# A decoder block on one core: second score passes over 128 partitions, three vectors loaded as rows, modulation sums kept in another order

## The chip, the core and the metric

The kernel runs on one core of one Trainium2 chip. The core has TensorE (PE: matmuls, with the weight loads, PEld, listed apart), VectorE (DVE), ScalarE (ACT), GpSimd (POOL) and SyncE (SP, which here only issues transfers). Each engine works through its own instructions in order; semaphores hold an instruction until what it needs is there. The metric is the time of one execution on the device in microseconds (us), from the first to the last instruction and what the launch adds.

## The reference

One layer on x of 512 tokens and width 2048, all in float32:

```
mod = silu(c) @ W_ada + b_ada              # six vectors of 2048: shift, scale, gate for mixer and MoE
h   = RMSNorm(x) * (1 + scale_mix) + shift_mix
q_a k_a v_a | q_b k_b v_b f_b = h @ W_in
o_a = sliding-window attention (128), 16 query heads on 4 key heads, ALiBi, sinks
o_b = forgetting attention, 16 heads: logits + cum[q] - cum[k], cum = cumsum(log sigmoid(f_b))
x   = x + gate_mix * ([RMSNorm(o_a) | RMSNorm(o_b)] @ W_out)
h2  = RMSNorm(x) * (1 + scale_moe) + shift_moe
x   = x + gate_moe * MoE(h2)               # top 1 of 4 groups, then top 2 of 8 experts
y   = RMSNorm_final(x)
```

Heads are 64 wide. The scores have to be as exact as float32 makes them, so the kernel cuts operands into a high part (the type fp32r, which PE takes in one pass) and a low part (what is left).

## The kernel before

**Start (0 to 155 us).** `load_x` brings x in four transfers of 1 MB on SP's queue; `rms_x` makes the row sums of squares on ACT and DVE. ACT's queue brings c, two parts of b_ada and norm_mix_g (lines 97 to 102), the latter three with `cols8`, that is, as runs of two numbers for each partition. Eight units of `gemv` then multiply pieces of W_ada (tiles `raws`, six buffers) with silu(c) on DVE, POOL and PE, and give the shift and scale of the mixer (`shA`, `scA`), 256 columns at a time; the queries and keys of the first heads are accumulated behind them.

**The turn (145 to 186 us).** `evac_k` takes each bank of keys out of PSUM. The high part goes to both halves of the partitions (`dst`, four ACT copies of 64 partitions), the low part to one half alone (`low`, two DVE subtractions): head e of a pair has its low part on partitions 64e to 64e+63. `evac_q` puts the high part of q on the same half and its low part on the other. Then the values of the sliding-window heads are projected (tiles `va`), and the logarithms of the forget gates are taken and summed (`log_forget`, `cumulate`, `cumulated`).

**Attention (186 to 750 us).** `attend` goes through units. A unit of the sliding-window heads (`swa_units`, 32 units) is one head and half of the tokens: two blocks of queries; a unit of the forgetting heads (`fox_units`, 64) is one head and one block of queries. `a1` makes the scores: a first matmul of q (128 partitions: high and low part) with the high part of k, and a second of q with the low part of k, over the 64 partitions `rows`. In a fox unit a third matmul in bf16 adds the causal mask. `a2` scales the probabilities of the unit before, `b` transposes those of two units before, `c` multiplies with the values. For each fox head `pre` spreads the cumulated logarithms over the partitions with a matmul (tile `bp`) over 48 partitions. Between these steps, `fill.take(step)` writes matmuls of the remaining projections (`transposed`, `natural`) into PE's order, and with them, at a fixed rate, the steps of a side work, `ada_side`: for the sections 3 and 4 of W_ada (shift and scale of the MoE, eight sums) and 2 (gate) it multiplies pieces of W_ada (tiles `raw`, five buffers, shared with the weights of the projections) with silu(c): row j=0 of a piece on DVE (`ga`, line 608), row j=1 on ACT and POOL (`gb`, lines 610 and 611). `finish` sums over the partitions by matmuls with `ones` (tile `cm`): for sections 3 and 4 four matmuls whose stationary operand is every fourth column of the sum, since the result is wanted with column p*4+j at partition p.

**Output and MoE (750 to 1950 us).** W_out, the gates of section 5, routing, then 16 pairs of experts. Nothing in it is changed but the place of one small transpose and of its two loads: `norm_a` put `grow` (the gains of the output norms) through PE into `gout`; `small_loads` loads it on SP's queue.

The order is written out by hand throughout (a manual schedule). Each transfer signals one of eight semaphores (DMAHW0 to DMAHW7) in turn, and a later transfer on the same one waits until the earlier has landed.

## Time and profile before

| | |
|---|---|
| median of 3 runs | 1953.34 us (1949.9 to 1963.09) |
| the profiled execution | 1952.11 us, of which the span 1950.4 us |
| PE busy | 1853.0 us (95%) |
| DVE busy | 1085.3 us (56%) |
| ACT busy | 824.5 us (42%) |
| POOL busy | 347.7 us (18%) |
| HBM read | 566.78 MB |

The span runs from the first to the last instruction. "Busy" of PE counts from a matmul's start to its modelled end, and matmuls overlap, so a PE that is 100% busy may still run at half of its pace: the distance from one start to the next is what a matmul costs in a chain of them. Rows of the timeline give start and duration in us; an "x8" is eight instructions merged into one row, from the first start to the last end.

### The profile page before, as it was taken

The numbers are of one execution on the slowest core, as the hardware profiler recorded it, in microseconds if no ns is written. First come the engines' busy times: TensorE is split into PE (matmuls) and PEld (weight loads), VectorE is DVE, ScalarE is ACT, GpSimd is POOL, SyncE is SP. The second block draws the span as 40 slices with busy tenths as digits, with TensorE's granted clock in tenths as the row PEclk, the third lists the DMA queues.
The fourth block names the chain that finished last, engine by engine and source line by source line (L and its number), as shares of the span: only waits on it lengthen the run. The fifth ranks groups of instructions, "written<-read, shape, count | busy, mean of one in ns | idle before, by whom it ended". The sixth has DMA issues, their size and how long they took to land.

```text
span 1950.4 us, 25464 instructions
## 1 busy us (share of the span) xinstructions
PE 1853.0 (95%) x9287; PEld 1122.2 (58%) x9287; DVE 1085.3 (56%) x2046; ACT 824.5 (42%) x1710; POOL 347.7 (18%) x281
## 2 busy tenths in 40 slices
PE   4999999999999999997999999999999999999994
PEld 2668777787777777875344444444444444444442
DVE  5775777767777555656344445444544445444435
ACT  4445655555555433444433334333333333333313
POOL 2440433443344321453000000000000000000000
PEclk9999999999999999998999999999999999999998
DMA  9994454565566332767799998999999999999994
GB/s 313 327 290 106 147 159 139 173 205 159 170 198 191 105 119 79 237 219 308 287 421 379 383 380 353 385 411 406 422 416 412 412 410 421 406 415 414 410 410 151
DMA packets 211749, 572.73 MB, mean 294 GB/s; under 512 B 25721, under 2 KB 113817, under 8 KB 162977
## 3 DMA queue, kind: packets, MB, share of 16 engines
q1 hardware_dynamic: 207632, 570.96, 78.4%
q8 instruction: 75, 1.23, 0.3%
q10 hardware_dynamic: 3984, 0.07, 0.1%
q14 instruction: 58, 0.47, 0.1%
HBM read 566.78 MB, written 4.19 MB: 293 GB/s over the span
## 4 chain that ended last, share of the span: by engine, by line
PE 84%; DVE 7%; ACT 3%; DMA 2%; issue 2%; POOL 1%; ACTq 1%; SPq 0%; DVEq 0%; POOLq 0%
PE pg L1371 12%; PE pu L1371 11%; PE y L1394 11%; PE xg L1351 7%; PE o L1416 5%; PE qp L216 3%; PE qp L217 3%; PE qp L218 3%; PE xe L1359 2%; DMA raw<-in_w_ada_dram 2%; PE vb L216 2%; PE vb L217 2%; PE vb L218 2%; PE sb L776 1%; DVE sum L291 1%
## 5 line engine op out<-in xcount | busy, mean ns | idle before, releaser
L1419 DVE SCALAR_TENSOR_TENSOR x<-o,wpair,x 128x512 f32<-128x512 f32 x240 | 163.5, 744 | 239.2 <-PE o L1416 239.2
L1371 PE MATMUL pg<-w,cw 128*64 128x512 f32 x1008 | 231.6, 602 | 1.2 <-ACT cw L1361 1.2
L1371 PE MATMUL pu<-w,cw 128*64 128x512 f32 x1008 | 227.3, 592 | 0.0
L611 POOL TENSOR_TENSOR gb<-gb,raw 128x512 f32<-128x512 f32 x112 | 163.1, 1456 | 288.8 <-ACT raw L610 237.3
L1394 PE MATMUL y<-w,cw 128*64 128x512 f32 x960 | 210.0, 594 | 0.1
L1361 ACT ACTIVATE cw<-xe,shM,scM 128x128 f32<-128x128 f32 x256 | 96.2, 456 | 248.0 <-PE xe L1359 247.8
L1340 DVE SCALAR_TENSOR_TENSOR wlo<-x,rs,whi 128x512 fp32r<-128x512 f32 x252 | 172.3, 746 | 43.3 <-ACT whi L1334 43.3
L1334 ACT ACTIVATE whi<-x,rs 128x512 fp32r<-128x512 f32 x256 | 163.4, 711 | 1.1 <-DVE rs L136 1.1
L1371 PEld LDWEIGHTS pu<-w,cw 128*64 128x64 f32 x1008 | 73.4, 137 | 142.9 <-issue 141.9
L1371 PEld LDWEIGHTS pg<-w,cw 128*64 128x64 f32 x1008 | 67.1, 137 | 130.3 <-issue 123.5
L1394 PEld LDWEIGHTS y<-w,cw 128*64 128x64 f32 x960 | 67.4, 137 | 129.3 <-issue 123.6
L1400 DVE TENSOR_TENSOR cw<-y,gm 128x512 f32<-128x512 f32 x60 | 41.5, 692 | 152.9 <-PE y L1394 150.8
L178 DVE TENSOR_TENSOR wlo_s<-raw,whi_s 128x512 fp32r<-128x512 f32 x96 | 85.6, 892 | 73.3 <-ACT whi_s L177 73.2
L608 DVE SCALAR_TENSOR_TENSOR ga<-raw,csil,ga 128x512 f32<-128x512 f32 x112 | 108.8, 972 | 24.8 <-DMA raw<-in_w_ada_dram 24.4
L1351 PE MATMUL xg<-wlo,cr 128*128 128x512 f32 x256 | 104.7, 409 | 7.5 <-DVE wlo L1340 7.5
L1351 PE MATMUL xg<-whi,cr 128*128 128x512 f32 x256 | 107.3, 419 | 1.4 <-DVE cr L1314 1.4
L216 PE MATMUL qp<-hT_hi,whi_s 128*128 128x512 f32 x256 | 108.5, 424 | 0.0
L1352 ACT ACTIVATE cw<-xg 128x512 f32<-128x512 f32 x64 | 38.2, 598 | 165.9 <-PE xg L1351 165.9
L217 PE MATMUL qp<-hT_lo,whi_s 128*128 128x512 f32 x256 | 100.9, 394 | 0.0
L218 PE MATMUL qp<-hT_hi,wlo_s 128*128 128x512 f32 x256 | 100.6, 393 | 0.0
L610 ACT ACTIVATE raw<-raw,csil 128x512 f32<-128x512 f32 x112 | 79.6, 712 | 32.0 <-DMA raw<-in_w_ada_dram 29.6
L1407 ACT ACTIVATE mr<-cw 128x512 fp32r<-128x512 f32 x30 | 18.9, 632 | 165.1 <-DVE cw L1400 141.1
(421 smaller groups left out, 3601.6 us busy)
## 6 DMA issues: line engine op xcount, KB each, us to landing
w<-in_w_gate_dram SPq DMA_DIRECT2D x126, 1024.0 KB, 8.5
w<-in_w_up_dram SPq DMA_DIRECT2D x126, 1024.0 KB, 12.4
w<-in_w_down_dram SPq DMA_DIRECT2D x126, 1024.0 KB, 11.1
raw<-in_w_ada_dram SPq DMA_DIRECT2D x128, 512.0 KB, 4.1
raws<-in_w_ada_dram SPq DMA_DIRECT2D x64, 512.0 KB, 5.8
raw<-in_w_in_dram SPq DMA_DIRECT2D x160, 128.0 KB, 3.1
raw<-in_w_out_dram SPq DMA_DIRECT2D x32, 512.0 KB, 4.3
raw<-in_w_in_dram SPq DMA_DIRECT2D x48, 256.0 KB, 3.5
```

Of the source, the lines that this page charges most:

```text
L216: PE.matmul(o, lhi, rhi, start=first, stop=False, **kw)
L217: PE.matmul(o, lhi, rlo, start=False, stop=False, **kw)
L218: PE.matmul(o, llo, rhi, start=False, stop=last, **kw)
L608: V.scalar_tensor_tensor(a, ts[n][:, j, :], s, a, op0=OP.mult, op1=OP.add)
L611: G.tensor_add(a, a, ts[n][:, j, :])
L1334: S.activation(hi, x1[cc][:, tb, :], AF.Identity, scale=rs[:, tb:tb + 1])
L1340: V.scalar_tensor_tensor(lo, x1[cc][:, tb, :], rs[:, tb:tb + 1], hi.bitcast(F32), op0=OP.mult, op1=OP.subtract)
L1351: PE.matmul(g, self.oh[:, tb, :], v, start=i == 0, stop=i == len(self.parts) - 1)
L1371: PE.matmul(o[64 * e:64 * e + 64, :], XE[:, cc, j, 64 * e:64 * e + 64], w[cc, e][:, j, :], start=cc == 0 and j == 0, stop=cc == 3 and j == 3)
L1394: PE.matmul(ys[dc][64 * e:64 * e + 64, :], self.ht[:, k, 64 * e:64 * e + 64], self.wd[k, e][:, dc, :], start=k == 0, stop=k == 3)
L1416: PE.matmul(os_[tb], self.ohT[:, tb, :], v, start=i == 0, stop=i == 1)
L1419: V.scalar_tensor_tensor(x2, os_[tb], self.w_col(tb), x2 if self.n else x1[dc][:, tb, :], op0=OP.mult, op1=OP.add)
```

## The change

Four things are done.

1. `evac_k` makes `low` for both halves of the partitions, as `dst` is: each subtraction is followed by an ACT copy to the other half. The second score matmul of `swa_units` and `fox_units` then runs over all 128 partitions. `kTl` becomes two tiles, and the tile `l` of `heads2` doubles. The cumulated logarithms are likewise put in tiles of 128 columns, so that `bp` is a matmul over 128 partitions (96 of them zeros).
2. `bsh` and `gmix` are loaded as 24 rows of 256 (`vrow`) and transposed on PE into `vecs`; `grow` is loaded and transposed at the start as well.
3. `ada_side` writes the sums of sections 3 and 4 with j ahead of p: the operand t is read with a step of four numbers (16 bytes), on DVE and POOL. The stationary operands of `cm` are then 128 numbers in a row.
4. `ones` becomes one column that is read with step zero.

```diff
+    vrow = sb.tile([24, 256], F32, tag="bias", name="vrow", bufs=2)
+    for n, v in enumerate((b_ada[0:D], b_ada[D:2 * D], norm_mix_g)):
+        S.dma_start(vrow[8 * n:8 * n + 8, :], v.rearrange("(u f) -> u f", u=8))
...
-    ones = big.tile([128, 128], F32, name="ones")
-    V.memset(ones, 1.0)
+    ones1 = big.tile([128, 1], F32, name="ones1")
+    V.memset(ones1, 1.0)
+    ones = ones1.to_broadcast([128, 128])
...
+    vt = ps.tile([128, 2, 24], F32, tag="tr", name="vt")
+    for j in range(2):
+        PE.transpose(vt[:, j, :], vrow.rearrange("r (p j) -> r j p", j=2)[:, j, :], ident[:24, :24])
+    V.tensor_copy(vecs.rearrange("p n (u j) -> p n u j", j=2), vt.rearrange("p j (n u) -> p n u j", n=3))
...
         for e, here, there in HALVES:
-            V.tensor_sub(low[here, :], acc[here, :], dst[here, e, :].bitcast(F32))
+            V.tensor_sub(low[here, e, :], acc[here, :], dst[here, e, :].bitcast(F32))
+            S.activation(low[there, e, :], low[here, e, :].bitcast(F32), AF.Copy)
...
-                    PE.matmul(cp[:, j:j + 1], acc.rearrange("q (p j) -> q j p", j=4)[:, j, :], ones[:, 0:1],
+                    PE.matmul(cp[:, j:j + 1], acc[:, j * 128:(j + 1) * 128], ones[:, 0:1],
...
+                    t = ts[n][:, j, :]
+                    if sec in (3, 4):
+                        a, t = a.rearrange("q (j p) -> q j p", j=4), t.rearrange("q (p j) -> q j p", j=4)
...
-                        V.scalar_tensor_tensor(a, ts[n][:, j, :], s, a, op0=OP.mult, op1=OP.add)
+                        V.scalar_tensor_tensor(a, t, s, a, op0=OP.mult, op1=OP.add)
...
-                        G.tensor_add(a, a, ts[n][:, j, :])
+                        G.tensor_add(a, a, t)
...
-    cum = sb.tile([128, TB, 48], F32, tag="q0", name="cum")
+    cum = sb.tile([128, TB, 128], F32, tag="q0", name="cum")
...
-                            PE.matmul(s[:, b, :w], q[rows, sl], kl[rows, k0:k0 + w], start=False, stop=True)
+                            PE.matmul(s[:, b, :w], q[:, sl], kl[:, k0:k0 + w], start=False, stop=True)
...
-                            PE.matmul(bp, pick[:, h:h + 1].to_broadcast([48, 128]), cumT, start=True, stop=True)
+                            PE.matmul(bp, pick[:, h:h + 1].to_broadcast([128, 128]), cumT, start=True, stop=True)
...
-                            PE.matmul(s[:, :w], q[rows, e, sl], kl[rows, :w], start=False, stop=False)
+                            PE.matmul(s[:, :w], q[:, e, sl], kl[:, e, :w], start=False, stop=False)
```

Three places of the order move. First the head of ACT's queue, before:

```order
L97 DMA ccol<-in_c_dram 128x4x4
L100 DMA bsh<-in_b_ada_dram 128x8x2 x2
L102 DMA gmix<-in_norm_mix_g_dram 128x8x2
L116 ACT_TABLE_LOAD
L116 ACTIVATE csig<-ccol 128x16 [waits DMAHW0_49]
```

and after:

```order
L95 DMA ccol<-in_c_dram 128x4x4
L99 DMA vrow<-in_b_ada_dram 8x256 x2
L99 DMA vrow<-in_norm_mix_g_dram 8x256
L114 ACT_TABLE_LOAD
L114 ACTIVATE csig<-ccol 128x16 [waits DMAHW0_49]
L252 DMA grow<-in_out_norm_swa_g_dram 8x128
L253 DMA grow<-in_out_norm_fox_g_dram 8x128
```

The three loads in runs of two numbers are gone; two loads that stood on SP's queue at the turn stand behind the first activation.

Second, the head of SP's queue, before:

```order
L249 DMA xt_102<-in_x_dram 128x2048
L249 DMA xt_103<-in_x_dram 128x2048
L249 DMA xt_104<-in_x_dram 128x2048
L249 DMA xt_105<-in_x_dram 128x2048
L282 DMA raws<-in_w_ada_dram 128x4x256 [waits DMAHW0_49]
```

and after:

```order
L262 DMA xt_102<-in_x_dram 128x2048
L262 DMA xt_103<-in_x_dram 128x2048
L262 DMA xt_104<-in_x_dram 128x2048 [waits DMAHW0_49]
L262 DMA xt_105<-in_x_dram 128x2048 [waits DMAHW1_49]
L295 DMA raws<-in_w_ada_dram 128x4x256 [waits DMAHW2_49]
```

With two more transfers ahead of them, the third and fourth quarter of x now wait on semaphores 0 and 1 (those of c and of the first quarter of x).

Third, ACT's order where the keys leave PSUM (`evac_k`, called twice), before:

```order
L471 ACTIVATE kTa<-acc_0_111 64x512 [waits PE_49]
L472 ACTIVATE kTa<-acc_0_111 64x512
L471 ACTIVATE kTa<-acc_0_111 64x512
L472 ACTIVATE kTa<-acc_0_111 64x512
L471 ACTIVATE kTa<-acc_1_112 64x512 [waits PE_49]
L472 ACTIVATE kTa<-acc_1_112 64x512
L471 ACTIVATE kTa<-acc_1_112 64x512
L472 ACTIVATE kTa<-acc_1_112 64x512
L177 ACTIVATE hi_s_1417<-raw 128x544 [waits DMAHW7_49,DMAHW0_49,Activation_49]
```

and after:

```order
L482 ACTIVATE kTa<-acc_0_111 64x512 [waits PE_49]
L483 ACTIVATE kTa<-acc_0_111 64x512
L482 ACTIVATE kTa<-acc_0_111 64x512
L483 ACTIVATE kTa<-acc_0_111 64x512
L486 ACTIVATE kTl_q_1412<-kTl_q_1412 64x512 [waits DVE_49] x2
L482 ACTIVATE kTa<-acc_1_112 64x512 [waits PE_49]
L483 ACTIVATE kTa<-acc_1_112 64x512
L482 ACTIVATE kTa<-acc_1_112 64x512
L483 ACTIVATE kTa<-acc_1_112 64x512
L486 ACTIVATE kTl_l_1413<-kTl_l_1413 64x512 [waits DVE_49] x2
L175 ACTIVATE hi_s_1433<-raw 128x544 [waits DMAHW2_49,DMAHW1_49,Activation_49]
```

Twice two copies that wait for DVE stand ahead of the next bank and ahead of `hi_s`, the high part of the next weights; the eight `evac_k` of the forgetting heads get the same two copies each. PE's own order in attention is the same instruction for instruction.

## Rows read from the trace of the kernel before

**Rows 1.** Busy time of each engine by stage (windows): PE, PEld, DVE, ACT, POOL with the number of instructions, then the granted clock, the DMA share and GB/s.

```profile
186.00:352.00 166.00, 164.77 (x919) 129.19 (x919) 124.58 (x354) 97.14 (x277) 59.81 (x44) 0.98 0.52 151
352.00:530.00 178.00, 178.00 (x978) 141.05 (x977) 126.75 (x259) 99.62 (x211) 78.22 (x54) 0.99 0.61 181
530.00:750.00 220.00, 217.93 (x1157) 166.68 (x1156) 137.33 (x264) 104.04 (x211) 82.22 (x61) 0.98 0.47 143
750.00:915.00 165.00, 149.63 (x739) 121.62 (x738) 107.94 (x154) 71.48 (x120) 67.68 (x44) 0.98 0.66 228
915.00:1930.00 1015.00, 994.33 (x4540) 455.92 (x4540) 460.50 (x756) 364.30 (x717) 0.00 (x0) 0.99 0.95 387
```

**Rows 2.** PE's timeline in a unit of the sliding-window heads: two blocks of queries, with a matmul of the projections (L216 to L218) behind them.

```profile
306.12 0.28 PE L709 MATMUL sa<-kTa,qTa 128*128 128x256 f32 x1
306.33 0.38 PE L710 MATMUL sa<-kTl,qTa 64*128 64x256 f32 x1
306.64 0.39 PE L709 MATMUL sa<-kTa,qTa 128*128 128x256 f32 x1
306.95 0.38 PE L710 MATMUL sa<-kTl,qTa 64*128 64x256 f32 x1
307.26 0.39 PE L216 MATMUL vb<-whi_s,hT_hi 128*128 128x256 f32 x1
307.49 0.28 PE L217 MATMUL vb<-wlo_s,hT_hi 128*128 128x256 f32 x1
307.61 0.28 PE L218 MATMUL vb<-whi_s,hT_lo 128*128 128x256 f32 x1
```

**Rows 3.** The weight loads (PEld) at the same place, on the same clock.

```profile
306.01 0.19 PEld L709 LDWEIGHTS sa<-kTa,qTa 128*128 128x128 f32 x1
306.33 0.18 PEld L710 LDWEIGHTS sa<-kTl,qTa 64*128 64x128 f32 x1
306.64 0.19 PEld L709 LDWEIGHTS sa<-kTa,qTa 128*128 128x128 f32 x1
```

**Rows 4.** PE's timeline in a unit of the forgetting heads with 512 keys.

```profile
616.42 0.39 PE L775 MATMUL sb<-k,q 128*128 128x512 f32 x1
616.74 0.50 PE L776 MATMUL sb<-l,q 64*128 64x512 f32 x1
617.17 0.23 PE L777 MATMUL sb<-causal_b,ident_b 128*128 128x128 bf16 x1
617.21 0.36 PE L216 MATMUL vb<-whi_s,hT_hi 128*128 128x256 f32 x1
```

**Rows 5.** All second score matmuls and all weight loads of `cm` (by source line): duration min/median/max in ns, first and last start in us, forms with counts.

```profile
L710 PE MATMUL sa<-kTl,qTa x64: 323/380/579, 180.2 to 354.6; 64*128 64x256 f32 x48, 64*128 64x128 f32 x16
L776 PE MATMUL sb<-l,q x64: 322/410/502, 360.3 to 730.4; 64*128 64x128 f32 x16, 64*128 64x256 f32 x16, 64*128 64x384 f32 x16, 64*128 64x512 f32 x16
L574 PEld LDWEIGHTS cm<-ones,ga x64: 308/329/332, 243.5 to 523.6; 128*128 128x128 f32 x64
```

**Rows 6.** PE's timeline at one `cm` (eight matmuls merged; the stationary operand has a step of 16 bytes), and at a sum of the same shape whose stationary operand is 128 numbers in a row (L900), followed by a `bp` and by full matmuls of the projections.

```profile
243.68 1.80 PE L574 MATMUL cm<-ones,ga 128*128 128x1 f32 x8
245.34 0.30 PE L709 MATMUL sa<-kTa,qTa 128*128 128x128 f32 x1
...
417.11 0.95 PE L900 MATMUL sp_a<-ones,ssq_a 128*128 128x1 f32 x8
417.99 0.23 PE L1005 MATMUL gps<-ident,grow 16*128 16x16 f32 x1
418.14 0.50 PE L766 MATMUL bp<-cumT,pick 48*128 48x512 f32 x1
418.57 0.50 PE L216 MATMUL qp<-hT_hi,whi_s 128*128 128x512 f32 x1
418.91 0.40 PE L217 MATMUL qp<-hT_lo,whi_s 128*128 128x512 f32 x1
419.14 0.40 PE L218 MATMUL qp<-hT_hi,wlo_s 128*128 128x512 f32 x1
```

**Rows 7.** DVE's additions into the modulation sums from 186 to 352 us (groups by line: count, busy us, mean ns, idle before), and by source line from 186 to 530 us (min/median/max ns).

```profile
L608 DVE SCALAR_TENSOR_TENSOR ga<-raw,csil,ga 128x512 f32<-128x512 f32 x27 | 24.0, 889 | 0.1
...
L608 DVE SCALAR_TENSOR_TENSOR ga<-raw,csil,ga x61: 735/746/1809, 193.3 to 525.1; 128x512 f32<-128x512 f32 x61
```

**Rows 8.** Two small DVE instructions of the routing on 128 numbers each: one reads them with a step of 32 bytes (L1209), one in a row (L1233).

```profile
L1209 DVE TENSOR_REDUCE ein<-emul 128x32 f32<-128x128 f32 x1 | 0.4, 378 | 0.0
...
L1233 DVE TENSOR_TENSOR place<-place,rk 128x128 f32<-128x128 f32 x1 | 0.3, 289 | 0.2 <-PE rk L1227 0.2
```

**Rows 9.** The start: ACT's queue holding a transfer back (timeline), the landing of the quarters of x (by tile), and DVE's first sum of squares (timeline).

```profile
3.22 9.51 ACTq L102 DMA_DIRECT2D gmix<-in_norm_mix_g_dram  x1
...
DMA to landing us min/median/max: 12.0/12.0/12.0
...
15.35 0.69 DVE L257 CUSTOM_DVE_ANT_0 sqscr<-xt 128x512 f32<-128x512 f32 x1
```

**Rows 10.** The turn: ACT's and DVE's timelines where the keys leave PSUM.

```profile
150.01 0.59 ACT L471 ACTIVATE kTa<-acc 64x512 fp32r<-64x512 f32 x1
...
152.32 0.65 ACT L177 ACTIVATE hi_s<-raw 128x544 fp32r<-128x544 f32 x1
...
150.08 1.39 DVE L474 TENSOR_TENSOR kTl<-acc,kTa 64x512 fp32r<-64x512 f32 x2 [2.56 <-ACT kTa L472]
```

More of the change, by code (lines that the diff above doesn't have):

```diff
@@ L97 @@
     S.dma_start(ccol, cols4(c))
[L98 to L102 removed]
+    bsh = big.tile([128, 2, 16], F32, name="bsh")
+    vrow = sb.tile([24, 256], F32, tag="bias", name="vrow", bufs=2)
+    for n, v in enumerate((b_ada[0:D], b_ada[D:2 * D], norm_mix_g)):
+        S.dma_start(vrow[8 * n:8 * n + 8, :], v.rearrange("(u f) -> u f", u=8))
     ident = big.tile([128, 128], F32, name="ident")
@@ L241 @@
     acc0 = [ps.tile([128, 512], F32, tag=f"acc{i}", name=f"acc0_{i}") for i in range(6)]
+    vecs = big.tile([128, 3, 16], F32, name="vecs")
+    vt = ps.tile([128, 2, 24], F32, tag="tr", name="vt")
+    for j in range(2):
+        PE.transpose(vt[:, j, :], vrow.rearrange("r (p j) -> r j p", j=2)[:, j, :], ident[:24, :24])
+    V.tensor_copy(vecs.rearrange("p n (u j) -> p n u j", j=2), vt.rearrange("p j (n u) -> p n u j", n=3))
+    gmix = vecs[:, 2]
     QA = ((0, 512),)
     KA = ((1024, 256),)
+    gout = big.tile([128, 16], F32, name="gout")
+    grow = sb.tile([16, 128], F32, tag="bias", name="grow", bufs=2)
+    S.dma_start(grow[0:8, :], out_norm_swa_g.rearrange("(k p) -> k p", p=128))
+    S.dma_start(grow[8:16, :], out_norm_fox_g.rearrange("(k p) -> k p", p=128))
+    gps = ps.tile([128, 16], F32, tag="tr", name="gps")
+    PE.transpose(gps, grow, ident[:16, :16])
+    V.tensor_copy(gout, gps)
     sx4 = big.tile([128, TB, 4], F32, name="sx4")
@@ L311, in gemv @@
             if sec == 0:
-                V.tensor_add(shA[:, ks], cp, bsh[:, 0, ks])
+                V.tensor_add(shA[:, ks], cp, vecs[:, 0, ks])
             else:
-                V.scalar_tensor_tensor(scA[:, ks], cp, 1.0, bsh[:, 1, ks], op0=OP.add, op1=OP.add)
+                V.scalar_tensor_tensor(scA[:, ks], cp, 1.0, vecs[:, 1, ks], op0=OP.add, op1=OP.add)
                 V.tensor_mul(scA[:, ks], scA[:, ks], gmix[:, ks])
@@ L402, in small_loads @@
     def small_loads():
-        for n, s in ((2, 3), (3, 4)):
+        for n, s in ((0, 3), (1, 4)):
             SP.dma_start(bsh[:, n].rearrange("p (c j) -> p c j", j=4), cols4(b_ada[s * D:(s + 1) * D]))
         SP.dma_start(gmoe, cols4(norm_moe_g))
-        SP.dma_start(grow[0:8, :], out_norm_swa_g.rearrange("(k p) -> k p", p=128))
-        SP.dma_start(grow[8:16, :], out_norm_fox_g.rearrange("(k p) -> k p", p=128))
         SP.dma_start(brt[:, 0:4], bcast(b_group, 4))
@@ L451 @@
                     channel_multiplier=-1)
-    grow = sb.tile([16, 128], F32, name="grow")
     ident_b = sb.tile([128, 128], BF, name="ident_b")
@@ L473, in evac_k @@
         for e, here, there in HALVES:
-            V.tensor_sub(low[here, :], acc[here, :], dst[here, e, :].bitcast(F32))
+            V.tensor_sub(low[here, e, :], acc[here, :], dst[here, e, :].bitcast(F32))
+            S.activation(low[there, e, :], low[here, e, :].bitcast(F32), AF.Copy)
     kTa = fr.tile([128, 2, 2, T], F32R, tag="ga", name="kTa")
-    kTl = sb.tile([128, 2, T], F32R, tag="q1", name="kTl")
+    kTl = [sb.tile([128, 2, T], F32R, tag=t, name=f"kTl_{t}") for t in ("q1", "l1")]
     qTa = {}
@@ L485 @@
     for i in range(2):
-        evac_k(acc0[i], kTa[:, i], kTl[:, i])
+        evac_k(acc0[i], kTa[:, i], kTl[i])
     for _ in prev:
@@ L655, in cumulated @@
         fill.take(2.6)
-        t = bank([48, TB, 128], "cumT")
+        t = bank([128, TB, 128], "cumT")
         for tb in range(TB):
@@ L695, in a1 @@
                     def a1(u=u, h=h, half=half, e=e, g=g, hf=hf, bias=bias):
-                        q, k, kl = qTa[g, h // 2 % 2][:, h % 2, hf, :], kTa[:, g, hf, :], kTl[:, g, :]
-                        rows = slice(64 * hf, 64 * hf + 64)
+                        q, k, kl = qTa[g, h // 2 % 2][:, h % 2, hf, :], kTa[:, g, hf, :], kTl[g][:, hf, :]
                         if half == 0:
@@ L771, in a1 @@
                             q, k, kl = qk[p]
-                            rows, sl = slice(64 * e, 64 * e + 64), slice(n * 128, (n + 1) * 128)
+                            sl = slice(n * 128, (n + 1) * 128)
                             w = u.w = (n + 1) * 128
@@ L873, in heads2 @@
         q, k, kl = qks[i] = [sb.tile(s, F32R, tag=f"{t}{i % 2}", name=f"{t}_{i}")
-                             for t, s in (("q", [128, 2, T]), ("k", [128, 2, T]), ("l", [128, T]))]
+                             for t, s in (("q", [128, 2, T]), ("k", [128, 2, T]), ("l", [128, 2, T]))]
         yield from transposed(f"qp{i}", [lambda acc: evac_q(acc, q), lambda acc: evac_k(acc, k, kl)])
@@ L974, in out_first @@
                         yield 1.3
-    gout = big.tile([128, 16], F32, name="gout")
     wrf = wr.rearrange("p c j e -> p (c j) e")
@@ L1003, in norm_a @@
         norm_o("a")
-        gps = bank([128, 16], "gps")
-        PE.transpose(gps, grow, ident[:16, :16])
-        V.tensor_copy(gout, gps)
     def more_o(fill):
```

22 lines of the change are left out of this document (8 added, 14 removed).

## The prediction

> **What bounds the kernel now.** Read first the busy times by stage [rows 1]. From 186 to 750 us PE is busy 560.7 of 564 us, DVE 75%, 71% and 62% of the three stretches, ACT some 55%, POOL less than half. So in attention PE sets the pace: whatever shortens PE's chain there shortens the run, until the next engine is full. From 915 us on PE is busy 994 of 1015 us; that stage isn't touched and only starts earlier. From 750 to 915 us PE has gaps (149.6 of 165), for transfers issued within that stretch; it is not touched either. I take both as shifted whole.
>
> Then PE's timeline, to see whether its busy time is work. In a sliding-window unit [rows 2] two full matmuls of 256 columns in a chain are 0.12 us apart (307.49, 307.61), but 0.31 lie between a 64-partition pass and its neighbours on both sides. The weight loads [rows 3] show why: a full matmul's load stands ahead of it (306.01 for the matmul at 306.12); the load of a 64-partition matmul, and of the full one after it, begins in the same hundredth as the matmul (306.33, 306.64). The load of 0.18 us is then not hidden.
>
> **Score passes.** The chain of [rows 2] from 306.12 to 307.49 is five steps, 1.37 us; five steps of 0.12 are 0.60, so 0.77 us of a unit is exposed. All 64 second passes are two to a unit [rows 5], 32 units: 24.6 us. 16 of the passes have 128 columns, too short to hide a load completely; I take 24. In a forgetting unit [rows 4] the two steps from 616.42 to 617.17 are 0.75 us, against 2 x 0.23 for full matmuls of 512 columns (418.91 to 419.14 in [rows 6]): 0.29 us, times 64 [rows 5] 18.6; for the short ones again, 17. The bf16 mask behind them stays, and I assume that the change of type costs no more than now: its own successor comes after 0.04 us (617.17, 617.21).
>
> That the second pass reads 128 partitions instead of 64 costs PE nothing: the step goes by columns, as first and second passes of the same width show. The Trainium skill (TensorEngine Tiling (Array Packing), When to Use Tiling) speaks against the edit: a contraction of 64 or less should take half of the array, so that two run at once. By that rule nothing would be gained here and a possible overlap would be given up; the sum for these passes would be 0 instead of 41 us. The rows show no pair that overlaps, since a full pass stands on either side of each 64-partition one; the same page's Key Properties (changing the mode drains the engine) is what the trace agrees with, at 0.18 us for each load.
>
> **bp and cm.** A `bp` of 48 partitions has the same pattern [rows 6]: 0.43 us to its successor and 0.34 from there, against 0.23 and 0.23, 0.31 in all; 16 of them, 5 us. Eight matmuls of a `cm` take 243.68 to 245.34, 1.66 us; the same shape with its operand in a row 417.11 to 417.99, 0.88. Eight sums: 6.2 us, spread evenly over 243 to 524 us [rows 5, 6]. PE's sum is 24 + 17 + 5 + 6 = 52 us.
>
> Spread: 186 to 352 us has the sliding-window passes and three `cm`, 24 + 2 = 26. L776 runs from 360 to 730 us [rows 5], so 352 to 530 has some 46% of its gain and of `bp`, and five `cm`: 8 + 2 + 4 = 14. 530 to 750 has the rest, 9 + 3 = 12.
>
> **What is late next: DVE.** In the first stretch DVE's 124.6 us [rows 1] would lie in 165 - 26 = 139. And it gets dearer: of the 64 additions into the sums of sections 3 and 4 (eight sums, eight pieces), 27 of L608 and some four first products lie here [rows 7], and each now reads with a step of 16 bytes. No row of DVE has that step. The nearest is L1209 [rows 8], with 32 bytes: 378 ns against 289 for as many numbers in a row, 0.70 ns each, which would be 0.36 us on 512. Lower bound nothing, upper twice that, as one row of another operation can be off by that much. I take 0.36, since the weight loads of `cm` show that 16 bytes is already a bad step for PE. That is 31 x 0.36 = 11 us here and 33 x 0.36 = 12 in the next stretch. POOL's additions read with the same step. POOL is not full: 59.8 us of 166, 78.2 of 178 [rows 1]; 0.65 us more on each, half of what one takes on average in [rows 1] (59.81 by 44), leaves it below 60%. But DVE's additions last 889 ns on average where the shortest take 735 [rows 7], which I put down to POOL holding them up; an estimate of 4 to 5 us for each stretch covers that this grows.
>
> So DVE needs 124.6 + 11 + 4 = 140 us in the first stretch, more than PE. It now idles 41 us there, nearly all behind a slow PE; I leave it 10. The stretch then takes 150 instead of 166: **16 of 26 us are realized**. In the second DVE needs 126.8 + 12 + 5 = 144, with 10 idle 154, below PE's 178 - 14 = 164: all 14. In the third DVE has 137 of 208: all 12. Sum **42 us**.
>
> The 16 copies of the eight later `evac_k` are 0.59 us each [rows 10], 9.4 us of ACT over 400 us in which it is busy 55%, and the matmuls two units behind wait for nothing of theirs. I cost them at nothing; without that cover each `evac_k` would hold ACT about 2 us, 16 in all.
>
> **The turn.** In the order ACT's two new copies stand ahead of the second bank and ahead of `hi_s`, each waiting for DVE. The first subtractions end at 150.08 + 1.39 = 151.47; with the copy behind them the second bank starts at 152.06 instead of 150.01. Four copies to 154.5, subtractions to 155.9, the last copy to 156.5: `hi_s` comes 4.2 us late against 152.32 [rows 10]. Behind it in ACT's queue stand the queries' copies and the weights of the next projection, for which PE waits, and nothing there has slack. **Minus 4 us.** Nothing is the lower bound, 5 the upper.
>
> **The start.** A transfer of ACT's queue (L102) holds that queue for 9.51 us [rows 9], and the first activation with it; three rows of 1 KB a piece cannot. But x lands 12.0 us after its issue [rows 9], so that DVE's first sum of squares at 15.35 could be some 2 us earlier at most; and the third and fourth quarter of x now wait for semaphores that they didn't (see the order). Between minus 2 and plus 4, I take **plus 2**. Transposes and copies of `vecs` and `gout` hide behind that same landing. `ones` with step zero costs nothing.
>
> Sum: 42 - 4 + 2 = 40 us. The profiled execution took 1952.1 us and would take 1912; the median of the runs shown is 1953.3, so **1913 us**.
>
> **Rivals.**
> - *The step is free on DVE and all of PE's 52 us are realized*: DVE then needs 130 of 139 us. 52 - 2 = 50, 1903 us. For it: the low share of the other engines. Against it: L1209, and two engines at 93% and 100% that wait for each other. 0.2.
> - *The step costs twice as much*: DVE needs 124.6 + 22 + 5 = 152 us in the first stretch, with 10 idle 162: 4 us gained; in the second 126.8 + 24 + 6 = 157, 167: 11. With 12 and minus 2 that is 25, 1928 us. The Trainium skill (GPSIMD Engine Reference, Performance pitfalls for Q7 kernels) has a rule to this effect for POOL: reads with a step of more than 8 bytes cost some half more for each element. No run shows it so far. 0.14.
> - *The 64 partitions are not what exposes the load* (first and second pass load the same q again): then only `cm` gains, 6 - 2 = 4 us, 1949. For it: in the score passes nothing in the rows tells the two apart. Against it: `bp` loads something else and shows the same. 0.05.
> - *Slower*: the steps bind DVE. In the first two stretches it has 251.3 us of work; with the 12 us of the third and minus 2, the change loses as soon as these stretches grow by 10, to 354 us. With 20 idle that is 251 + 64p = 334, p = 1.3 us, nearly thrice a normal addition. At 2 us it would be 251 + 128 + 20 = 399, 45 more than that, 1998 us. Against it: L1209 at 0.7 ns a number. 0.04.
>
> **The numbers.** My forecast has 0.57, its own range 1906 to 1921. The range to 8 in 10 takes in the free step below (1903, with the start at its best 1899) and the dear step above (1928). A change of 1% (19.5 us) is about what a measurement of this kernel can tell from none. Faster by more: the forecast and the first two rivals, less a little for what I have not seen, 0.88; within: the third and that rest, 0.08; slower 0.04.
>
> **What would show it.** Steps of 0.12 and 0.23 us around the second passes, with loads ahead of the matmuls; `cm` in 0.9 us; PE no longer full between 186 and 352 us, with waits for DVE or ACT; DVE's additions near 1.1 us; `hi_s` of the turn some 4 us later against the keys. It would be wrong if the loads stay exposed, if the additions stay at 0.74 us and DVE has room, or if ACT's waits for DVE in `evac_k` stop PE in the forgetting heads.

## The result and the profile after

The changed kernel takes 1976.3 us (median of four runs, 1973.7 to 1978.8) against 1951.6 us of the kernel before beside it (1948.0 to 1963.1): ratio 1.0108, interval 1.0082 to 1.0134. It is slower by 1.1%, where 1913 us were forecast. The profiled execution took 1973.7 us, with a span of 1972.0.

First the same stages by the clock, with the columns of [rows 1]:

```profile
186.00:352.00 166.00, 147.48 (x886) 121.06 (x885) 141.29 (x339) 92.50 (x268) 70.89 (x43) 0.95 0.49 143
352.00:530.00 178.00, 156.24 (x901) 126.80 (x901) 140.30 (x245) 95.50 (x203) 86.52 (x49) 0.96 0.54 163
530.00:750.00 220.00, 211.18 (x1180) 169.01 (x1179) 148.14 (x288) 115.83 (x238) 89.93 (x61) 0.98 0.53 160
```

PE has fallen from 164.8 to 147.5 and from 178.0 to 156.2 us, but it does fewer instructions in that time (886 against 919), so it isn't ahead: it waits. DVE has risen in each. Both kernels issue the same instructions in the same order on PE in attention, but for the one small transpose into `gout`, which stands in stretch 2 before and at the start after. So the same work can be cut out of both: from the first sliding-window score to the first forgetting score, from there to the last `cm`, and on to the last forgetting score. Before, and then after:

```profile
180.10:360.20 180.10, 178.03 (x1006) 140.39 (x1004) 132.19 (x375) 108.44 (x298) 65.74 (x48) 0.98 0.51 151
360.20:523.60 163.40, 163.40 (x895) 128.68 (x894) 117.59 (x239) 90.83 (x191) 73.86 (x51) 1.00 0.63 188
523.60:730.40 206.80, 204.84 (x1090) 157.00 (x1090) 132.24 (x261) 100.41 (x207) 76.21 (x53) 0.98 0.49 149
```

```profile
182.80:375.40 192.60, 166.16 (x1005) 136.65 (x1003) 158.97 (x376) 107.75 (x298) 79.52 (x48) 0.94 0.48 141
375.40:545.40 170.00, 156.17 (x894) 126.47 (x894) 134.73 (x237) 92.85 (x197) 87.35 (x52) 0.98 0.59 176
545.40:749.10 203.70, 194.88 (x1092) 156.35 (x1091) 135.92 (x264) 106.22 (x217) 79.56 (x54) 0.97 0.51 155
```

Stretch 1 grew by 12.5 us, stretch 2 by 6.6, stretch 3 shrank by 3.1. (They are called so below.)

The score passes did become what the prediction said. PE's timeline in a sliding-window unit answers to [rows 2], its weight loads to [rows 3], a forgetting unit to [rows 4], a `cm` to [rows 6]:

```profile
199.26 0.33 PE L724 MATMUL sa<-kTa,qTa 128*128 128x256 f32 x1
199.43 0.28 PE L725 MATMUL sa<-kTl_q,qTa 128*128 128x256 f32 x1
199.55 0.28 PE L214 MATMUL vb<-whi_s,hT_hi 128*128 128x256 f32 x1
...
199.32 0.19 PEld L725 LDWEIGHTS sa<-kTl_q,qTa 128*128 128x128 f32 x1
199.44 0.19 PEld L214 LDWEIGHTS vb<-whi_s,hT_hi 128*128 128x128 f32 x1
...
638.39 0.39 PE L791 MATMUL sb<-l,q 128*128 128x512 f32 x1
638.63 0.23 PE L792 MATMUL sb<-causal_b,ident_b 128*128 128x128 bf16 x1
...
244.60 0.95 PE L586 MATMUL cm<-ones,ga 128*128 128x1 f32 x8
```

The load of the second pass begins at 199.32, ahead of its matmul at 199.43, and the next matmul follows after 0.12 us, where it was 0.31; 0.24 (638.39 to 638.63) where it was 0.43; eight matmuls of a `cm` end after 0.95 us, where it was 1.80.

So why is PE late? What PE waited for, from the first sliding-window score to the last `cm` (waits of PE: line, releaser, us in total, times, longest), some 40 us in all, of which the five largest rows are shown; the kernel before waits 2.0 us there in all:

```profile
PE oa L760 <- ACT pta L750: 8.0, 4, 2.9
PE vb L214 <- ACT whi_s L175: 5.0, 3, 2.9
PE bp L781 <- ACT pta L750: 5.0, 1, 5.0
PE tb L810 <- DVE ptb L814: 3.5, 1, 3.5
PE vb L215 <- DVE wlo_s L176: 2.9, 5, 0.9
```

And ACT and DVE, which PE waits for, wait for each other. Waits in stretch 1, first of the kernel before (DVE three rows, ACT one), then of the one after:

```profile
DVE wlo_s L178 <- ACT whi_s L177: 16.0, 17, 1.7
DVE wlo_s L184 <- ACT whi_s L183: 11.8, 11, 2.9
DVE pa L713 <- PE sa L710: 6.3, 10, 1.6
...
ACT pa L716 <- DVE nma L713: 62.2, 31, 3.9
```

```profile
DVE wlo_s L176 <- ACT whi_s L175: 13.6, 14, 2.0
DVE wlo_s L182 <- ACT whi_s L181: 7.7, 11, 1.4
...
ACT pa L731 <- DVE nma L728: 79.4, 30, 4.9
```

The prediction makes no use of this view. Of DVE's 47.9 us of idle time before, only 6.3 end with a score of PE; 27.8 end with ACT's high part of a weight piece (`whi_s`), which DVE needs for the low part (`wlo_s`). With PE faster the 6.3 all but vanish, and the 27.8 fall only to 21.3. ACT on its side idles for DVE's maxima (`nma`), 62.2 us before and 79.4 after. Each stands in its own queue behind something that the other has still to deliver.

DVE's groups in stretch 1, before and after (groups by line: count, busy us, mean ns, idle before; the first row answers to [rows 7]):

```profile
L608 DVE SCALAR_TENSOR_TENSOR ga<-raw,csil,ga 128x512 f32<-128x512 f32 x28 | 25.5, 911 | 0.1
L184 DVE TENSOR_TENSOR wlo_s<-raw,whi_s 128x256 fp32r<-128x256 f32 x32 | 18.9, 631 | 11.9 <-ACT whi_s L183 11.8
L178 DVE TENSOR_TENSOR wlo_s<-raw,whi_s 128x512 fp32r<-128x512 f32 x20 | 15.4, 776 | 16.1 <-ACT whi_s L177 16.0
```

```profile
L623 DVE SCALAR_TENSOR_TENSOR ga<-raw,csil,ga 128x512 f32<-128x512 f32 x28 | 37.8, 1351 | 0.1
L182 DVE TENSOR_TENSOR wlo_s<-raw,whi_s 128x256 fp32r<-128x256 f32 x32 | 22.4, 739 | 7.8 <-ACT whi_s L181 7.7
L176 DVE TENSOR_TENSOR wlo_s<-raw,whi_s 128x512 fp32r<-128x512 f32 x20 | 19.6, 982 | 13.7 <-ACT whi_s L175 13.6
```

The additions took 12.3 us more. The splits, in which nothing was changed, took 7.7 us more: they lengthen where POOL is at work, as POOL's and DVE's timelines show at one place:

```profile
377.52 2.04 POOL L626 TENSOR_TENSOR gb<-gb,raw 128x512 f32<-128x512 f32 x1 [1.97 <-ACT raw L625]
...
378.84 1.27 DVE L176 TENSOR_TENSOR wlo_s<-raw,whi_s 128x512 fp32r<-128x512 f32 x1 [0.70 <-ACT whi_s L175]
```

POOL's addition ends at 379.56, DVE's subtraction at 380.11, 0.55 us later. Counted over the splits of 512 numbers up to the last `cm`: 30 begin while no instruction of POOL runs and last 0.69 us (0.67 to 0.71). 26 begin under one of POOL's additions of two tiles; they last 1.42 us on average, and each ends 0.54 to 0.60 us after that addition. The Trainium skill (SBUF — State Buffer, Who interferes with whom) says that a DVE instruction with two SBUF inputs contends with a GpSimd instruction that reads SBUF, and that the ports they share are an exclusive lock. These 26 agree. Five more begin under a first product of POOL (L621, which reads one tile in SBUF); they last 0.85 us on average and end 0.14 us after it at the latest, so for that instruction this trace does not show the same wait.

### The profile page after: what moved, and what is told of

It reads as the page before. It is cut to its first block, busy times and chain, and to the rows that moved or that the text cites. A ratio compares the mean times of both kernels' runs of the same rounds, so it can differ in the third digit from the quotient of the medians.

```text
span 1972.0 us, 25491 instructions
## 1 busy us (share of the span) xinstructions
PE 1829.2 (93%) x9289; PEld 1117.4 (57%) x9289; DVE 1131.9 (57%) x2048; ACT 834.2 (42%) x1730; POOL 376.8 (19%) x281
## 4 chain that ended last, share of the span: by engine, by line
PE 66%; DVE 12%; ACT 6%; issue 4%; DMA 3%; POOL 1%; SPq 0%; DVEq 0%; ACTq 0%; POOLq 0%
PE pg L1382 12%; PE pu L1382 11%; PE y L1405 11%; PE xg L1362 6%; PE o L1427 5%; DVE ga L623 3%; PE xe L1370 2%; DMA raw<-in_w_ada_dram 2%; PE qp L214 2%; PE qp L216 2%; PE qp L215 2%; DVE wlo_s L176 1%; ACT raw L625 1%; ACT whi_s L175 1%; PE ob L822 1%
## 5 line engine op out<-in xcount | busy, mean ns | idle before, releaser
L626 POOL TENSOR_TENSOR gb<-gb,raw 128x512 f32<-128x512 f32 x112 | 183.9, 1642 | 292.1 <-ACT raw L625 238.9
L623 DVE SCALAR_TENSOR_TENSOR ga<-raw,csil,ga 128x512 f32<-128x512 f32 x112 | 131.2, 1171 | 26.9 <-DMA raw<-in_w_ada_dram 26.0
L176 DVE TENSOR_TENSOR wlo_s<-raw,whi_s 128x512 fp32r<-128x512 f32 x96 | 96.9, 1010 | 74.5 <-ACT whi_s L175 74.2
L1363 ACT ACTIVATE cw<-xg 128x512 f32<-128x512 f32 x64 | 38.2, 597 | 164.7 <-PE xg L1362 164.7
L216 PE MATMUL qp<-hT_hi,wlo_s 128*128 128x512 f32 x256 | 102.0, 398 | 0.0
L797 ACT ACTIVATE pb<-pb,nmb 128x128 f32<-128x128 f32 (+1 forms) x64 | 36.0, 562 | 127.8 <-DVE nmb L795 121.5
```

The source lines that it names most:

```text
L176: V.tensor_sub(lo, src, hi.bitcast(F32))
L216: PE.matmul(o, llo, rhi, start=False, stop=last, **kw)
L623: V.scalar_tensor_tensor(a, t, s, a, op0=OP.mult, op1=OP.add)
L626: G.tensor_add(a, a, t)
```

## The experiments

Medians, each beside runs of the kernel before on the same chip (1953 to 1956 us each time); R is the ratio to it, with its interval.

**1. The sums in rows again.**

```diff
-                    if sec in (3, 4):
-                        a, t = a.rearrange("q (j p) -> q j p", j=4), t.rearrange("q (p j) -> q j p", j=4)
...
-                    PE.matmul(cp[:, j:j + 1], acc[:, j * 128:(j + 1) * 128], ones[:, 0:1],
+                    PE.matmul(cp[:, j:j + 1], acc.rearrange("q (p j) -> q j p", j=4)[:, j, :], ones[:, 0:1],
```

> The changed kernel with part 3 taken back: the modulation sums are read and written in rows again, and cm reads its stationary operand with a step of 16 bytes as before; score passes, loads as rows and ones stay. If the stepped additions eat the gain (theory A): DVE's additions back at 0.75 us in the median, PE over 95% busy from 186 to 545 us, and 1905 to 1925 us. If PE has become faster than the softmax work of DVE and ACT can follow, steps or not (theory B): PE still waits some 30 us for ACT and DVE there, and 1935 to 1955 us. If the new copies in evac_k are what costs (theory C): 1955 us or more.

1942.1 us, R 0.9942 (0.9925 to 0.9958): 34 us below the changed kernel (32 by the ratios). The step is the largest share, but theory A is not the whole: the time lies in B's range, 17 us above A's. The signs are mixed too: DVE's additions are back at a median of 0.75 us, as A has it, while PE still waits 19 us for ACT and DVE up to 560 us, less than B's 30.

**2. The step alone**, on the kernel before (the inverse of the diff above).

> The kernel before with part 3 alone: sums of sections 3 and 4 read with a step of 16 bytes, cm in rows. Theory A: the additions alone fill DVE, PE waits without any other change, 1965 to 1990 us. Theory B: with the slow score passes left in, PE stays the slower one and covers the additions; cm gives 6 us back, 1945 to 1955 us. Theory C: the same, 1945 to 1955 us.

1970.4 us, R 1.0080 (1.0064 to 1.0097): slower by 16 us though PE keeps its slow passes. DVE had no such room in the kernel before either.

**3. and 4. The step on DVE alone, and on POOL alone.**

```diff
-                    if sec in (3, 4):
+                    if sec in (3, 4) and j == 0:
...
+                G.tensor_add(acc.rearrange("q (j p) -> q j p", j=4), acc.rearrange("q (j p) -> q j p", j=4),
+                             acc1.rearrange("q (p j) -> q j p", j=4))
```

(The merge shown is that of run 3, which reads POOL's sum with the step; `cm` reads in a row there, as in the change. For POOL `j == 1`; the merge reads POOL's sum with a step of 128 numbers and writes in rows, and `cm` reads with the step of 16 bytes as before.)

> The changed kernel with the step on DVE's additions alone; POOL adds in rows, and one merge for each sum reads with the step. If what counts is the time that DVE's own additions take (theory A1): 1960 to 1976 us. If what counts is POOL's longer additions, which hold DVE up (theory A2): DVE's other instructions return to their times of before and the run to 1915 to 1935 us. Theory B: 1940 to 1976 us.

> The changed kernel with the step on POOL's additions alone; DVE adds in rows, one merge for each sum writes with the step, and cm reads with the step as before. Theory A1: DVE has its room back, 1910 to 1930 us. Theory A2: 1955 to 1976 us, with DVE's instructions at L176 still near 1.0 us. Theory B: 1940 to 1960 us.

1960.7 us, R 1.0027 (1.0016 to 1.0038), and 1959.2, R 1.0033 (1.0018 to 1.0049): each is some 17 to 19 us above run 1, about half of the 34 us, so neither A1 nor A2 alone. (Both lie in theory B's wide ranges as well, so B is not told apart from them here.) With the step on POOL alone DVE's additions are back at a median of 0.75 us, and yet the splits on L176 take 1035 ns on average from 186 to 530 us, against 898 with the sums in rows.

**5. The copies of the low part later.** The sums are in rows; the copies are put in a list, from which one is taken behind each further piece of a projection.

```diff
-            S.activation(low[there, e, :], low[here, e, :].bitcast(F32), AF.Copy)
+            later.append(lambda e=e, here=here, there=there: S.activation(
+                low[there, e, :], low[here, e, :].bitcast(F32), AF.Copy))
...
+                        if m and copies:
+                            copies.pop(0)()
```

> As the run with the sums in rows (1942.1 us), but the two copies of the low part in each evac_k are issued later on ACT, one at a time behind the next pieces of the projection, so that none stands at the head of ACT's queue waiting for DVE; at the turn they stand behind the splits of the value weights. The same work, another place. If the waits of PE behind each evac_k (5.25 us at 347, 2.9 at 523) and the 4 us of the turn come from these copies: the first score 4 us earlier against the keys, no wait over 3 us behind an evac_k, and 1922 to 1932 us. If they come from DVE and ACT being too full for the faster PE: 1937 to 1943 us.

1932.1 us, R 0.9879 (0.9856 to 0.9902): 10 us below run 1 (12 by the ratios), on the upper edge of what was expected. From the keys to the first score it is 33.0 us (36.6 in run 1, 32.5 before). What the copies did is seen in run 1, in ACT's and PE's timelines at the first `evac_k` of the forgetting heads:

```profile
347.41 0.59 ACT L483 ACTIVATE k<-qp 64x512 fp32r<-64x512 f32 x1
348.75 1.35 ACT L486 ACTIVATE l<-l 64x512 fp32r<-64x512 f32 x2 [0.75 <-DVE l L485]
350.13 0.72 ACT L623 ACTIVATE raw<-raw,csil 128x512 f32<-128x512 f32 x1
350.76 0.61 ACT L175 ACTIVATE whi_s<-raw 128x512 fp32r<-128x512 f32 x1
351.39 0.60 ACT L682 ACTIVATE oT<-oa 128x512 f32<-128x512 f32 x1
351.89 0.48 ACT L748 ACTIVATE pta<-ta 128x384 f32<-128x384 f32 x1
...
347.18 0.28 PE L216 MATMUL vb<-whi_s,hT_lo 128*128 128x256 f32 x1
352.42 0.80 PE L779 MATMUL bp<-cumT,pick 128*128 128x512 f32 x1 [4.97 <-ACT pta L748]
```

The two copies and the wait ahead of them hold ACT from 348.00 to 350.10. Behind them stands, fourth in the queue, `pta` of the last sliding-window unit, for which PE waits 4.97 us. With the copies later that wait is 2.7 us.

**6. Only the last addition of a sum with the step**, into a fresh tile, so that `cm` is in rows.

```diff
+                rows, acc = acc, pool.tile([128, 512], F32, tag="gacc", name=f"gj_{sec}_{g}", bufs=2)
+                G.tensor_add(acc.rearrange("q (j p) -> q j p", j=4), rows.rearrange("q (p j) -> q j p", j=4),
+                             acc1.rearrange("q (p j) -> q j p", j=4))
```

> As the run with the copies late, and cm reads 128 numbers in a row as in the change, but only the last addition of each sum (POOL, one of eight pairs) reads with the step, into a fresh tile. If the step costs by the number of instructions that read with it: 0.7 us less on each cm for PE, 3 to 6 us below the run with the copies late, 1917 to 1928 us. If any stepped read of POOL is enough to upset DVE: no gain over it, 1925 to 1940 us.

1936.4 us, R 0.9913 (0.9891 to 0.9935): no gain over run 5. It is inconclusive on the step, since the fresh tile takes the second buffer: DVE's first product of the next sum had to wait for POOL's merge, 5.5 us in two of them (3.5 the longest), each merge lasting 2.14 us.

**7. DVE's time without the step.** The sums are in rows, copies as in the change.

```diff
+                        if sec in (3, 4):
+                            V.tensor_scalar(a[:, 0:384], a[:, 0:384], 1.0, None, op0=OP.mult)
```

> As the run with the sums in rows (1942.1 us), with a multiplication by 1.0 of 384 numbers behind each addition of DVE into the sums of sections 3 and 4: it adds work of about 0.36 us to DVE and no step. If the step costs by DVE's time alone: the same as the run with the step on DVE alone (1960.7 us), 1955 to 1966 us. If the stepped read does harm beyond its own time: 1942 to 1950 us.

1964.3 us, R 1.0045 (1.0023 to 1.0066), 22 us above run 1 and 4 above run 3. The multiplications added more than was meant: 0.36 us in the median, but 0.77 on average, since 24 of the 56 begin under an operation of POOL on two tiles; these last 1.31 us on average and end 0.21 to 0.22 us after it. By the windows DVE is busy 14.6 us longer than in run 1 in stretch 1 and 15.4 in stretch 2; the step on DVE alone (run 3) makes it 12.6 and 14.6. So about as much busy time of DVE costs about as much without the step as with it (22 us here; 19 in run 3, where `cm` gains besides), and the step need do no harm of its own.

**8. The change with the copies later**: the sums with the step, as changed, and the edit of run 5.

> The changed kernel, steps and all, with the copies of the low part issued later as above. If the copies cost by holding ACT's queue: 8 to 15 us below the changed kernel, 1961 to 1968 us. If with DVE full the copies lie in time that ACT waits anyway: only the turn's 4 us, 1970 to 1975 us.

1964.1 us, R 1.0048 (1.0032 to 1.0065): 12 us below the change. The copies hold ACT's queue whether DVE is full or not.

**9. and 10. POOL's time: writes and reads.** On run 1, behind POOL's additions for sections 3 and 4:

```diff
+                        if sec in (3, 4):
+                            G.memset(t, 0.0)
```

or `G.tensor_copy(t[:, 0:370], t[:, 0:370])`.

> As the run with the sums in rows (1942.1 us), with a memset of the 512 numbers that POOL has just added, behind each of its additions for sections 3 and 4: about 0.5 us of POOL's time each that only writes. If POOL's stepped additions cost 17 us because DVE's instructions with two SBUF operands wait for a POOL instruction that reads SBUF: no reading here, the splits (L176) stay near 0.8 us on average and the time at 1940 to 1947 us. If any time of POOL costs (its own order, or its writes): 1952 to 1965 us, as with the step on POOL alone.

> The same with a copy in place of 370 numbers instead of the memset: about the same 0.5 us of POOL's time each, but it reads SBUF. If it is the reading that holds DVE up: twice the added time of the step on POOL, so the splits above 0.95 us on average and 1955 to 1975 us. If any time of POOL costs: the same as the run with the memset, within 4 us. If neither costs: 1940 to 1947 us, and the step on POOL alone cost by something of its own.

1941.1 us, R 0.9929 (0.9907 to 0.9952), and 1948.0, R 0.9969 (0.9954 to 0.9985). The memsets (56 of 538 ns) cost nothing; the copies (56 of 662 ns) cost 6 us, and the splits on L176 take 901 ns on average with the former, 936 with the latter (898 in run 1). 1941.1 is what was expected if only POOL's reading holds DVE up; 1948.0 lies in none of the ranges. The traces agree on the reading: 8 splits of 512 numbers begin under a memset and last 0.69 us, as when POOL is idle; 7 begin under a copy and last 0.83. This fits the rule of the Trainium skill (SBUF — State Buffer, Who interferes with whom) for GpSimd instructions that only write. But the copies cost a third of the step's 17 us for more time of POOL's. The traces show part of the reason: in run 10 few splits meet a copy, while in run 4 24 splits begin under one of POOL's additions and last 1.46 us, against 23 of 1.17 us in run 1. Whether the stepped reading also holds DVE up beyond the longer time of the addition was not tried.

**11. and 12. Side work spread otherwise**, on run 5: a lower rate throughout, then a lower one in the sliding-window heads alone.

```diff
-    RATE, LAST_FILL, LAST = 200 / 275, 52.0, 5
+    RATE, LAST_FILL, LAST = 180 / 275, 52.0, 5
...
-         fox_units((i - 4,), qks, vbs) if i < 10 else last6[:LAST], lambda i=i: Fill(fills(i), side, RATE), total(i),
+         fox_units((i - 4,), qks, vbs) if i < 10 else last6[:LAST], lambda i=i: Fill(fills(i), side, 0.6 if i < 4 else 0.76), total(i),
```

> As the run with the copies late (1932.1 us), with the side work at nine tenths of its rate, so that its steps are spread over more of the attention heads and DVE has less to do from 186 to 530 us. If what is left of PE's waits comes from DVE's share of the side work: 3 to 8 us less, 1924 to 1929 us. If it comes from the chain of each unit (scores, DVE, ACT, transposes) whatever DVE's load: 1930 to 1935 us; slower if the gates of section 2 come too late.

> As the run with the copies late (1932.1 us), with the side work at 0.60 steps a microsecond (0.73 before) in the sliding-window heads and 0.76 in the forgetting heads, so that its end comes in time. If DVE's load sets the first stretch: the last sliding-window score 6 us earlier than with the copies late, as with the slower side work (336 against 342 us), some of it kept, and 1923 to 1929 us. If the load only moves the waits to the next stretch: 1930 to 1935 us.

1952.4 us, R 0.9997 (0.9980 to 1.0014), and 1939.8, R 0.9916 (0.9901 to 0.9930): both misses. With the lower rate the last sliding-window score came at 336.2 us (342.2 in run 5), but then the gates of section 2 weren't ready and PE stood 18.8 us for them at 646. With the shifted rate the 6 us that it is ahead when eight forgetting units are through (405.4 against 411.4) are lost eight units later (447.3 against 444.7).

**13. to 15. Is DVE's idle time room?** On run 5, for sections 3 and 4: more work for ACT, less for ACT, less for DVE.

```diff
+                            S.activation(ts[n][:, j, 0:128], ts[n][:, j, 0:128], AF.Copy)
...
-                        S.activation(ts[n][:, j, :], ts[n][:, j, :], AF.Copy, scale=s)
+                        if sec not in (3, 4):
+                            S.activation(ts[n][:, j, :], ts[n][:, j, :], AF.Copy, scale=s)
...
+                    elif j == 0 and sec in (3, 4):
+                        pass
```

> As the run with the copies late (1932.1 us), with one more ACT copy in place of 128 numbers behind each scaling of a piece for sections 3 and 4: 56 instructions of about 0.3 us, 28 of them in the sliding-window stretch of 173 us, where ACT is busy 107 us. If DVE and ACT work in one chain (theory P): the stretch grows by 5 to 9 us, the whole by 9 to 16 us, 1941 to 1948 us. If ACT has slack (theory Q): at most 2 us in the stretch, 1930 to 1936 us.

> As the run with the copies late, but ACT's scaling of the odd rows by silu(c) is left out for sections 3 and 4, so their sums lack this factor: ACT has 0.71 us less at 56 places, DVE and POOL do what they did. Theory P: the sliding-window stretch shrinks by 8 to 18 us from 173, the whole to 1905 to 1922 us. Theory Q: 1928 to 1933 us.

> As the run with the copies late, but DVE's additions for sections 3 and 4 (all but the first product of each sum) are left out, so their sums lack seven of eight even rows: DVE has some 50 us less in the two stretches. If DVE's load is what keeps PE from its gain (theories P and Q): PE over 97% busy in both stretches, the sliding-window stretch down to 153 to 160 us and the run to 1905 to 1915 us. If PE's gain was over-estimated: PE full and still over 165 us there, 1925 us or more.

1939.8 us, R 0.9925 (0.9908 to 0.9943); 1926.2, R 0.9850 (0.9824 to 0.9877); 1913.8, R 0.9790 (0.9773 to 0.9808). Stretch 1 (windows, columns as above) of run 5, then of the run with less for ACT, then all three stretches of the one with less for DVE:

```profile
178.70:351.80 173.10, 161.95 (x1004) 137.19 (x1004) 137.74 (x376) 106.99 (x298) 66.80 (x48) 0.95 0.52 156
```

```profile
179.30:345.40 166.10, 156.97 (x1005) 133.14 (x1003) 139.30 (x376) 89.89 (x269) 65.52 (x49) 0.98 0.55 165
```

```profile
178.70:337.00 158.30, 155.15 (x1006) 133.27 (x1004) 111.96 (x350) 108.14 (x300) 62.24 (x48) 0.98 0.56 168
337.00:492.80 155.80, 154.09 (x894) 127.98 (x893) 93.67 (x209) 96.51 (x198) 72.25 (x52) 1.00 0.66 199
492.80:690.30 197.50, 192.62 (x1089) 155.59 (x1090) 132.69 (x260) 105.28 (x214) 75.44 (x52) 0.98 0.51 156
```

Neither P nor Q as they stood. ACT's 17.1 us less shorten the stretch by 7.0, though ACT is idle a third of it; 8.2 us more lengthen it by 2.8. So in this stretch between a third and four tenths of what was taken from ACT or added to it shows in the length. In stretch 2 no such share is seen: 158.3 us in run 5, 160.2 with more for ACT and 160.3 with less. Without DVE's additions (run 15) PE is busy 98% and the stretch 21.8 us shorter than before: PE's gain is real, and DVE kept it back.

Set side by side, stretch 1 of all runs (length, DVE busy, DVE idle, in us, from the windows):

| kernel | length | DVE busy | DVE idle |
|---|---|---|---|
| before | 180.1 | 132.2 | 47.9 |
| the step alone, slow passes (2) | 194.6 | 155.1 | 39.5 |
| the change | 192.6 | 159.0 | 33.6 |
| step on DVE alone (3) | 184.8 | 150.8 | 34.0 |
| step on POOL alone (4) | 182.0 | 147.8 | 34.2 |
| DVE's time without the step (7) | 187.4 | 152.7 | 34.7 |
| the change, copies late (8) | 192.4 | 158.8 | 33.6 |
| sums in rows (1) | 173.4 | 138.1 | 35.3 |
| copies late (5) | 173.1 | 137.7 | 35.4 |
| last addition with the step (6) | 173.6 | 138.1 | 35.5 |
| POOL writes, POOL reads (9, 10) | 173.1, 177.3 | 137.8, 141.2 | 35.3, 36.1 |
| side work slower (11) | 165.1 | 131.7 | 33.4 |
| side work shifted (12) | 169.6 | 129.5 | 40.1 |
| more for ACT (13) | 175.9 | 137.7 | 38.2 |
| less for ACT (14) | 166.1 | 139.3 | 26.8 |
| less for DVE (15) | 158.3 | 112.0 | 46.3 |

With fast score passes and ACT's instructions as they are, the stretch lasts as long as DVE is busy plus 33 to 36 us in eleven of these kernels, whatever fills DVE from 132 to 159 us. Run 12, where DVE has least to do among these, is the exception with 40.1; there, as in run 11, 5 to 6 us end with PE's scores again. Only less work for ACT lowers that idle time clearly; without DVE's additions PE sets the pace again, and it rises. In stretch 2 DVE's idle time is 34 to 36 us only where it is busy for 132 us or more (with fast passes the change and runs 3, 7 and 8); in runs 1 and 5, busy 117 and 116, it is 42.

## Why the prediction was wrong

**PE's sum: right but for some 7 us.** The steps came as read from [rows 2] to [rows 4] and [rows 6]. With DVE's additions left out (run 15), the three stretches are 21.8, 7.6 and 9.3 us shorter than before, 38.7 in all, without the gain of `cm`; the sum without `cm` was 46. PE's busy time falls by 44.4 us there, so most of the 7 is waiting that is left. The rule of the Trainium skill that spoke against it (TensorEngine Tiling (Array Packing), When to Use Tiling) did not decide here: the passes of 128 partitions stand 0.12 us apart.

**The price of the step on DVE: right in size.** 0.36 us was taken, from L1209 [rows 8]. Up to the last `cm` the median of 60 additions is 1143 ns, against 746 [rows 7]: 0.40. On POOL it was over-estimated: 0.65 us was taken, and the medians are 1562 and 1304 ns, 0.26 or a fifth. The rival's rule for POOL in the Trainium skill (GPSIMD Engine Reference, Performance pitfalls for Q7 kernels), some half more for each element, asks for more than this trace shows: a fifth where one of two operands is read with the step, and a third for the first products, which read one (2069 ns against 1567 in the median).

**What it does to DVE's other work: too low in stretch 1.** 11 + 4 us were forecast there, 26.8 came (132.2 to 159.0); 12 + 5 in stretch 2, where 17.1 came. Of the 12 us too few 7.7 are the splits, most of which wait for POOL; the prediction looked for POOL's effect on the additions alone.

**The step that failed: "It now idles 41 us there, nearly all behind a slow PE; I leave it 10."** This put nearly all of DVE's idle time down to PE without a reason from the rows. 6.3 us were behind PE's scores and 27.8 behind ACT, by the waits of the kernel before shown above. In the stretches used here (stretch 1 is 14 us longer than the window of the prediction, with 6.5 us more of idle time) the forecast was 132 + 15 + 16.5 = 164 us; it became 159.0 + 33.6 = 192.6. With fast passes and no step at all (run 1) 35.3 us of idle time stay, where the forecast left 16.5. In stretch 2 it was 163.4 - 14 = 149, and became 134.7 + 35.3 = 170.0. With an idle time of 34 us the forecast's own DVE work would have given 181 us for stretch 1, no gain at all. The slower rival stood on the same idle time: it let the change lose from 1.3 us an addition, with 20 us of idle time in two stretches; it lost at 0.40, with 69.

**The copies of `evac_k`: costed at nothing, they cost 10 to 12 us** with the turn's 4. The prediction named the price without cover (2 us each time); the cover holds only in part, since what stands behind them in ACT's queue can be what PE needs next (seen at the first of the eight, 5 us of PE). Without any cover the eight in attention were to cost 16 us, and 6 to 8 came. In stretch 3, without steps, 12 us of gain were forecast; 3.1 came with the copies, 7.2 with the copies late (206.8 to 199.6).

**The turn and the start: right.** ACT's timelines at the turn and at the start, and DVE's first sum of squares (they answer to [rows 10] and [rows 9]):

```profile
147.93 0.60 ACT L483 ACTIVATE kTa<-acc 64x512 fp32r<-64x512 f32 x1
149.28 1.35 ACT L486 ACTIVATE kTl_q<-kTl_q 64x512 fp32r<-64x512 f32 x2 [0.75 <-DVE kTl_q L485]
150.65 0.59 ACT L482 ACTIVATE kTa<-acc 64x512 fp32r<-64x512 f32 x1
...
155.23 1.20 ACT L175 ACTIVATE hi_s<-raw 128x544 fp32r<-128x544 f32 x2
...
2.29 0.42 ACTq L99 DMA_DIRECT2D vrow<-in_norm_mix_g_dram  x1
...
12.00 0.68 DVE L270 CUSTOM_DVE_ANT_0 sqscr<-xt 128x512 f32<-128x512 f32 x1
```

`hi_s` comes 9.1 us behind the first `kTa` (146.12), against 4.7 before: 4.4 us late, 4.2 forecast. DVE's first sum of squares comes 3.35 us earlier (15.35 before), more than the 2 that the prediction gave as the most; of this 1.5 us reach the keys (147.59 before), 2 forecast.

**From 750 to 915 us** the change was to be shifted whole; it lost 4 us more there (the first `pg` is 22.7 us late, the sum of squares of the forgetting heads 18.6). With the sums in rows it is 2.2. What makes these was not tried and stays open.

The 63 us between 1913 and 1976, in medians: 34 for the step (run 1, with what `cm` gains by it already taken off) and 10 for the copies (run 5). The other 19 lie between run 5, at 1932, and 1913. In the prediction's own terms run 5 should even have come to some 1905: it has no step, no copies at the turn, and all of PE's sum but `cm`, 46 + 2 = 48 us. Of these 27 us, 18 come back when DVE's additions are left out (run 15, at 1914); they are what DVE's load keeps back even without the step and the copies. The 9 that are left are mostly the 7 of PE's sum.

## What to carry to other kernels

An engine's idle time is not all room. Read what ends it before it is given away: what ends with the engine that is to become faster goes, and what two helpers wait for each other mostly stays (here 6.3 us of 47.9 ended with PE, 12.6 went in run 1, and the forecast gave away 31). Work put on an engine that is 56% busy can still be on the path, by its own time and by what its queue holds back; an added instruction that waits for another engine belongs behind what the bound engine needs next. The best version measured here that computes the same is run 5, the changed kernel with the sums in rows and the copies late, 1.2% faster than before.
